# Both layers' attention recorded, and its instructions ordered on all five engines by measured durations

## Chip, cores, metric

One core of a Trainium2 chip. The metric is the device time of one execution in microseconds, as the median over runs. Five instruction streams run beside each other: TensorE (PE), VectorE (DVE), ScalarE (ACT), GpSimd (POOL) and SyncE (SP, which here issues the DMAs). Each runs its own instructions in the order in which the program lists them, and semaphores hold an instruction until its inputs are there.

## What is computed

A two-layer transformer trunk over 512 latent tokens and 256 context tokens, width 1024, all in float32. Each layer:

```python
h, hc = modulate(rms_norm(x, norm1)), modulate(rms_norm(ctx, norm1))
na_q, na_k, na_v, gq, gk, gv, ga, gb = split(h @ w_in)        # hc in the same way
ya = na_latent(...)   # 8 heads: 8x16 window on the 64-wide grid plus bias, and all context keys, one softmax
qb, kb = rope(rms_norm(heads(gq)) * q_gain), rope(rms_norm(heads(gk)) * k_gain)
yb = gqa_latent(...)  # 8 query heads on 2 key heads, latent and context keys
x = x + g1 * ((sigmoid(ga) * (ya @ w_pa) + sigmoid(gb) * (yb @ w_pb)) @ w_o)
if not last:          # context queries on context keys, same weights
    ctx = ctx + cg1 * branch_merge(ya_c, yb_c, ...)
x = x + g2 * swiglu(modulate(rms_norm(x, norm2)))             # ctx as well, if not last
```

## The kernel before

Products in float32 are made of three matmuls: each operand is split into a high and a low half (`wh`, `wl` of a weight, `h`, `hl` of the activations), and h by wh, hl by wh and h by wl add up in one PSUM bank (line L384). `wh` is an ACT copy (L369), `wl` the remainder, on POOL or DVE (L371).

`mixing` is one layer's attention: eight grouped-query heads (GQA), then eight neighbourhood heads (NA). Heads go through in items of two query blocks of 128. Of an item of GQA (`gqa_pair`) PE makes scores `sc` (L1040); DVE takes the minimum `m` over a row (L1048; the query is stored negated) and multiplies it by the row's reciprocal norm `r` (L1054, tile `hr`); ACT makes the exponential `p` and its sum (L1056); DVE scales p (L1010); PE transposes it into `tp` (L1066); ACT copies its high half `pth` (L1016) and DVE its low half `ptl` (L1017); PE multiplies both by the values into `y` (L1076), which ACT and DVE bring back (L1027). `ctx_item` does the same for context queries (L1098, L1103), `na_pair` for NA (L1167 to L1203).

`attend` interleaves one item's scores with the transposes and values of the two before it. In the gaps it runs *fillers*: projection blocks of the queries, keys, values and gates (`gq`, `nq`, `nk`, `nv`, `ga`, `gb`), which are PE work without a wait (tile `pj`) and write tiles that later items need (`kg`, `kk` for the GQA keys, `qg`, `q` for the queries, `qh` and `ql` for NA's). A query's rotation (`rope`) is a shuffle `sh`, a product with the sines on POOL (L791), one with the cosines (L792) and a sum on DVE (L793); a head's norm goes over a small power on POOL (`hr`, L807). A `bias` tile is loaded, zeroed in a part and subtracted on POOL (L1491, L1492).

The order of PE's instructions is planned while the program is built: `Flow` keeps a clock of PE and three timelines of ACT, DVE and POOL, on which each step books an estimated span:

```python
RATE = dict(a=(0.06, 0.00083, "a"), e=(0.28, 0.00083, "a"), v=(0.065, 0.00105, "v"), w=(0.065, 0.00058, "v"),
            g=(0.07, 0.00218, "g"), p=(0.0, 0.19, "g"))
```

A step that needs the result yields `Until(t)`, and the planner fills up to t. Numbers per layer stand in `PLAN` (which fillers in which order, hop times, a reserve). In the attention only PE's order is fixed by hand; DVE, ACT, POOL and SP get theirs from the framework's scheduler. The start of the kernel is ordered by hand on all engines, the feed-forward on PE, DVE and ACT.

After the attention, `merge` loads GQA's results back from memory (`yb`, L1555), splits them (`hi` L396, `lo` L397) and multiplies them by `wp` into `pp`; fillers that are left over run between the last values and the first `pp`. Meanwhile the modulation of the second norm is worked out from `crow` and `wmodT`.

## Time and profile before

| | |
|---|---|
| median of 3 runs | 1951.8 us (1947.15 to 1954.22) |
| the profiled execution | 1945.29 us, span 1943.5 us |
| mean granted clock of TensorE | 0.998 |
| PE busy | 1912.1 us, 98% of the span, 12298 instructions |
| DVE busy | 1470.0 us, 76% |
| ACT busy | 943.0 us, 49% |
| POOL busy | 226.6 us, 12% |
| DMA | 210.85 MB |

Stages in time: start to about 60 us, layer 0's attention to 416, its merge and feed-forward to 1130, layer 1's attention to 1452, the rest to 1943.

A row of a busy table or a group has an engine's busy time, the count in x, and the mean of one instruction in ns; "idle" is the time for which the engine stood just before that instruction, with what released it. PE's matmuls overlap, so that a row's own time is longer than the distance to the next one.

### The profile page before, as it was taken

The page shows a single profiled execution, that of the slowest core. Times are in us where ns is not written, and L with a number is a line of the kernel's source. Part 1 is how long each engine was busy: PE and PEld are TensorE (multiplying, and loading weights), DVE is VectorE, ACT ScalarE, POOL GpSimd, SP SyncE. Part 2 cuts the span into 40 slices and gives each one's busy share as a digit, 9 for nine tenths or more (in the row PEclk, how much of TensorE's full clock was granted, in tenths as well). Part 3 has the DMA queues.
Part 4 walks back from the last instruction along what each step waited for, and adds up shares of the span by engine and source line. Part 5 has one row for each costly group of instructions (what it writes and reads, how often), then busy time and mean ns, then how long its engine had stood idle before and what let it go on. Part 6 is the DMA issues. An engine that isn't in the chain of part 4 may idle for free.

```text
span 1943.5 us, 31493 instructions
## 1 busy us (share of the span) xinstructions
PE 1912.1 (98%) x12298; PEld 1775.8 (91%) x12298; DVE 1470.0 (76%) x2802; ACT 943.0 (49%) x1822; POOL 226.6 (12%) x131
## 2 busy tenths in 40 slices
PE   8999999999999999999999998999999999999998
PEld 8989999998899999999999888889988999999998
DVE  7468887769877888786868577888657687877785
ACT  5466666652336533342424346666553355544553
POOL 0332222213300000000000012322300000000000
PEclk9999999999999999999999999999999999999999
DMA  8121112235562233334344411112235532332332
GB/s 328 44 65 48 47 64 63 77 105 182 170 217 87 66 120 122 117 116 133 131 141 143 143 62 55 47 60 64 73 102 173 201 109 77 98 120 88 103 97 83
DMA packets 71669, 210.85 MB, mean 108 GB/s; under 512 B 8544, under 2 KB 10720, under 8 KB 71520
## 3 DMA queue, kind: packets, MB, share of 16 engines
q1 hardware_dynamic: 71520, 208.84, 33.5%
q8 instruction: 96, 1.57, 0.3%
q14 instruction: 53, 0.43, 0.1%
HBM read 196.75 MB, written 6.82 MB: 105 GB/s over the span
## 4 chain that ended last, share of the span: by engine, by line
PE 69%; DVE 4%; issue 1%; ACT 1%; POOL 0%; DMA 0%; DVEq 0%; POOLq 0%; ACTq 0%
PE po L384 21%; PE qu L1740 14%; PE pj L384 11%; PE qv L1740 7%; PE pp L384 4%; PE qc L1740 3%; PE pf L384 3%; PE pv L957 1%; PE sc L1040 1%; PE y L1076 1%; PE tp L1066 1%; PE y L1203 1%; PE sc L1167 1%; PE tp L1191 1%; DVE m L1048 0%
## 5 line engine op out<-in xcount | busy, mean ns | idle before, releaser
L1740 PE MATMUL qu<-r,w 128*128 128x384 f32 (+1 forms) x1872 | 295.9, 310 | 0.3
L1740 PEld LDWEIGHTS qu<-r,w 128*128 128x128 f32 x1872 | 281.0, 190 | 4.9 <-DVE tt L2219 3.7
L384 PE MATMUL pj<-h,wh 128*128 128x512 f32 (+1 forms) x704 | 257.4, 366 | 3.3 <-ACT kg L816 1.7
L384 PE MATMUL pj<-h,wl 128*128 128x512 f32 (+1 forms) x704 | 247.6, 352 | 1.2 <-POOL wl L371 1.2
L384 PE MATMUL pj<-hl,wh 128*128 128x512 f32 (+1 forms) x704 | 247.0, 351 | 0.0
L369 ACT ACTIVATE wh<-wr 128x1024 fp32r<-128x1024 f32 (+1 forms) x131 | 124.6, 954 | 168.9 <-issue 43.5
L1603 ACT ACTIVATE w<-wr 128x512 fp32r<-128x512 f32 x234 | 145.4, 625 | 107.6 <-DVE wr L2183 36.1
L384 PE MATMUL po<-ph,wh 128*128 128x512 f32 (+1 forms) x576 | 197.5, 343 | 0.0
L384 PE MATMUL po<-ph,wl 128*128 128x512 f32 (+1 forms) x576 | 196.9, 342 | 0.0
L384 PE MATMUL po<-pl,wh 128*128 128x512 f32 (+1 forms) x576 | 196.3, 341 | 0.0
L371 POOL TENSOR_TENSOR wl<-wr,wh 128x1024 fp32r<-128x1024 f32 (+1 forms) x67 | 151.0, 2258 | 370.8 <-ACT wh L369 364.7
L1595 DVE SCALAR_TENSOR_TENSOR x<-po,G,x 128x256 f32<-128x256 f32 (+3 forms) x168 | 99.2, 596 | 101.0 <-PE po L384 100.0
L1607 DVE TENSOR_TENSOR w<-wr,w 128x512 fp32r<-128x512 f32 x234 | 159.4, 686 | 11.9 <-ACT w L1603 11.0
L384 PEld LDWEIGHTS pj<-h,wl 128*128 128x128 f32 x704 | 133.3, 189 | 19.7 <-POOL wl L371 1.6
L1740 PE MATMUL qv<-r,w 128*128 128x384 f32 (+1 forms) x936 | 150.7, 310 | 0.3 <-ACT tt L1746 0.3
L384 PEld LDWEIGHTS pj<-h,wh 128*128 128x128 f32 x704 | 133.7, 190 | 17.4 <-ACT kg L816 1.9
L384 PEld LDWEIGHTS pj<-hl,wh 128*128 128x128 f32 x704 | 134.0, 190 | 13.5
L1740 PEld LDWEIGHTS qv<-r,w 128*128 128x128 f32 x936 | 141.2, 190 | 0.5 <-ACT tt L1746 0.5
L1016 ACT ACTIVATE pth<-tp 128x512 fp32r<-128x512 f32 x176 | 103.2, 595 | 65.1 <-PE tp L1066 36.8
L512 POOL TENSOR_TENSOR rs<-rs,expo 128x2 f32<-128x2 f32 (+2 forms) x8 | 6.2, 773 | 1100.4 <-DVE rs L511 1100.4
L1017 DVE TENSOR_TENSOR ptl<-tp,pth 128x512 fp32r<-128x512 f32 x176 | 119.4, 684 | 18.4 <-ACT pth L1016 17.0
L384 PEld LDWEIGHTS po<-ph,wl 128*128 128x128 f32 x576 | 108.3, 188 | 14.3 <-DVE wl L1911 0.4
(255 smaller groups left out, 4325.2 us busy)
## 6 DMA issues: line engine op xcount, KB each, us to landing
wr<-wfi SPq DMA_DIRECT2D x88, 512.0 KB, 3.3
wr<-wmodT SPq DMA_DIRECT2D x84, 512.0 KB, 3.4
wr<-win SPq DMA_DIRECT2D x68, 512.0 KB, 3.3
wr<-wfo SPq DMA_DIRECT2D x64, 256.0 KB, 2.7
wr<-wo SPq DMA_DIRECT2D x26, 512.0 KB, 3.9
wr<-wp SPq DMA_DIRECT2D x32, 256.0 KB, 3.0
x<-x SPq DMA_DIRECT2D x16, 384.0 KB, 6.7
wr<-wmod SPq DMA_DIRECT2D x12, 512.0 KB, 7.6
```

Source lines behind the costliest of these rows:

```text
L369: nc.scalar.activation(hi, raw, AF.Copy)
L371: (eng or nc.gpsimd).tensor_tensor(lo, raw, hi[:].bitcast(F32), op=ALU.subtract)
L384: nc.tensor.matmul(ps[:, : b - a], u[:, c], v[k][:, a:b], start=(k == 0 and i == 0), stop=(k == nk - 1 and i == 2),)
L957: nc.tensor.matmul(ps[:, t * 256 : t * 256 + 256], a[k][:, tok], b[:, c], start=(k == 0 and i == 0), stop=(k == KB - 1 and i == 2))
L1016: nc.scalar.activation(hi, tp, AF.Copy)
L1017: nc.vector.tensor_tensor(lo, tp, hi[:].bitcast(F32), op=ALU.subtract)
L1040: nc.tensor.matmul(s[:, lo:up], qt[:, b * P : (b + 1) * P], kk[k][:, lo:up], start=(k == 0 and (b % 2 == 0 or lo > 0)), stop=(k == 1), ski ...
L1066: nc.tensor.transpose(tp[:, (2 * j + b) * P : (2 * j + b + 1) * P], ps_[b][:, (k + j) * P : (k + j + 1) * P], self.ident)
L1595: self.nc.vector.scalar_tensor_tensor(x[j][:, f:u], ps[:, f - a : u - a], self.G[l][i][:, s, j : j + 1], x[j][:, f:u], op0=ALU.mult, op1=A ...
L1603: self.nc.scalar.activation(t[:, :n], src, AF.Copy)
L1607: self.nc.vector.tensor_tensor(t[:, n : 2 * n], src, t[:, :n].bitcast(F32), op=ALU.subtract)
L1740: nc.tensor.matmul(banks[bank], u[:, c], v, start=(first and k == 0 and i == 0), stop=(k == kn - 1 and i == 2), skip_group_check=True)
```

## The change

Both layers get `all=True`. Then every instruction that the attention issues goes through a proxy into a list (`Plan.add`) in place of the program. For each instruction the list holds its engine, a cost from measured durations (`cost`, `HOPS` between engines, `TAIL` for overlap), and which earlier instructions it must follow, found from the regions of tiles that it reads and writes; a PSUM bank counts as one region, so two uses of one bank by different engines follow each other. `Flow` takes the ends from these records instead of `RATE` (`Plan.go`). When all is recorded, `emit` runs a simulated list scheduler: PE and SP keep the recorded order; among DVE's, ACT's and POOL's ready instructions the one with the earliest due time goes first, where due times are reckoned back from PE's planned starts. A DVE instruction of the kinds tensor_tensor, tensor_scalar and copy without an operand in PSUM (`shared`) starts no earlier than POOL is free; a POOL instruction is put off when such a DVE instruction with an earlier due time would fall into it. Then the instructions are issued by planned start, and their order holds on all five engines.

Besides, m times r moves from DVE to ACT (64 single products in `gqa_pair`; 8 double ones become 16 in `ctx_item`), in `ctx_item` the scaling of p comes after both exponentials, and the rotation is booked when it is recorded. The numbers in `PLAN` stay.

```diff
+         busy=12, ctx=0.0, vat=(1, 1), load=2, qt=2, rx=2, slow=(1.1, 1.2, 1), banks="gst", lead=(2, 1, 2), quiet=0.0, spared=0, all=True),
...
     def go(self, t, *ops):
+        if self.plan:
+            return self.plan.go(t, ops)
...
+    def passed(self, v):
+        self.clock = max(self.clock + v, self.plan.pe if self.plan else 0.0)
...
+    def __getattr__(self, op):
+        run = getattr(getattr(self._engines.nc, self._name), op)
+        plan = self._engines.plan
+        return (lambda *a, **k: plan.add(self._name, op, run, a, k)) if plan else run
...
+    HOPS = dict(p=0.055, v=0.035, a=0.035, g=0.078, s=0.1)
+    TAIL = dict(p=-0.16, v=0.085, a=0.105, g=0.07, s=-2.2)
...
+    def go(self, t, ops):
+        flow, seen = self.flow, set()
+        for e, n in ops:
+            fixed, each, on = RATE[e]
+            if on in self.recent:
+                t = max(t, self.recent.pop(on))
+                seen.add(on)
+            elif on not in seen:
+                t += 0.05 + fixed + 0.08 + n * each
+        return t + flow.hop - 0.05
...
+        return (0, P, f // S * S, -(-g // S) * S) if psum else (p, p + ap.ap[0][1], f, g)
...
+    def cost(self, lane, op, aps, kw, psum):
+        n = self.size(aps[0])
+        scaled = hasattr(kw.get("scale"), "ap") + hasattr(kw.get("bias"), "ap")
+        if lane == "p":
+            wide = op != "transpose" and aps[1].dtype == F32
+            return max(0.05, 4 * n * PASS / P) if wide else max(PASS, FIX + n * 0.4167e-3)
+        if lane == "s":
+            return n * aps[0].ap[0][1] * 4 / 0.34e6
+        if lane == "g":
+            return 0.31 if op == "memset" else 0.5 + n * 0.142 if n <= 16 else 0.14 + n * 0.0022
+        if lane == "a":
+            return 0.16 + n * 0.00088 + 0.08 * scaled + 0.1 * ("accum_out" in kw)
+        if op == "tensor_reduce":
+            n = self.size(aps[1])
+        one = not psum and op in ("tensor_scalar", "tensor_copy", "reciprocal") and n > 16
+        return 0.15 + n * (0.0006 if one else 0.00105) + 0.06 * (op == "scalar_tensor_tensor" and not psum)
...
+        me = len(self.ops)
+        t, after = flow.clock - 6.0, set()
+        uses = [(v.name, self.region(v, b), any(v is o for o in outs), b) for v, b in zip(aps, bank)]
+        for tile, (p, q, f, g), mine, b in uses:
+            for ((p1, q1, f1, g1), wrote), (end, who) in self.parts.get(tile, {}).items():
+                if (mine or wrote or b) and p < q1 and p1 < q and f < g1 and f1 < g:
+                    who = {w for w in who if mine or wrote or self.ops[w]["lane"] != lane}
+                    if who:
+                        t = max(t, max(self.ops[w]["end"] for w in who if w != me) + self.HOPS[lane])
+                        after.update(who)
+        if lane == "p":
+            at = max([flow.clock, self.pe] + [self.ops[w]["end"] + self.HOPS["p"] for w in after if self.ops[w]["lane"] != "p"])
+            end = at + cost - self.TAIL["p"]
+            self.pe = at + cost
+        elif lane == "s":
+            at = max(t, self.dma)
+            self.dma = at + cost
+            end = self.dma + 2.2
+        else:
+            end = flow.lines[lane].take(t, cost - self.TAIL[lane]) + self.TAIL[lane]
+            at = end - cost
+            self.recent[lane] = max(self.recent.get(lane, 0.0), end)
+        self.ops.append(dict(lane=lane, op=op, cost=cost, after=after, run=run, args=args, kw=kw, at=at, end=end,
+                             shared=lane == "v" and not any(bank) and op in ("tensor_tensor", "tensor_scalar", "tensor_copy"),
+                             tiles={u[0] for u in uses}))
...
+        due, frees = [0.0] * n, [[] for _ in ops]
+        for key in room:
+            of = [t for t in self.users if rings.get(t) == key]
+            for t, new in zip(of, of[_Bufs.rings[of[0]][2] :]):
+                for u in self.users[t]:
+                    if u < self.users[new][0]:
+                        frees[u].append(self.users[new][0])
+        for i in reversed(range(n)):
+            o = ops[i]
+            due[i] = o["at"] if o["lane"] == "p" else min(
+                [due[j] - o["cost"] - 0.05 for j in then[i] + frees[i]], default=o["at"] + 15.0)
+        start, end, ready = [None] * n, [0.0] * n, [-9.0] * n
...
+        def begins(i):
+            if left[i]:
+                return None
+            t = max(ready[i], clock[ops[i]["lane"]])
+            for tile in opens[i]:
+                if not room[rings[tile]]:
+                    return None
+                t = max(t, min(room[rings[tile]]) + self.HOPS[ops[i]["lane"]])
+            return max(t, clock["g"] - 0.07) if ops[i]["shared"] else t
...
+        def put_off(i, t):
+            o = ops[i]
+            for u, j in sorted(soon):
+                if u < t + o["cost"] and due[j] < due[i] and u + ops[j]["cost"] + o["cost"] < due[i]:
+                    t = max(t, u + ops[j]["cost"])
+            return t
...
+            for e in "pavgs":
+                some = queue[e][:1] if e in queue else can[e]
+                times = [(t, i) for i in some for t in (begins(i),) if t is not None]
+                if e == "g":
+                    times = [(put_off(i, t), i) for t, i in times]
+                if times:
+                    first = min(times)[0]
+                    d, t, i = min((due[i], t, i) for t, i in times if t <= first + 0.1)
+                    if e in "av":
+                        for u, j in times:
+                            took = ops[j]["cost"]
+                            if due[j] < d and u < t + ops[i]["cost"] and due[i] > u + took:
+                                d, t, i = due[j], u, j
+                    if best is None or (t, i) < best[:2]:
+                        best = t, i, e
...
+            t, i, e = best
+            o = ops[i]
+            start[i] = t
+            end[i] = t + o["cost"] - min(self.TAIL[e], 0.0)
+            clock[e] = t + o["cost"] - max(self.TAIL[e], 0.0)
+            if e == "a" and o["kw"].get("accum_out") is not None and not exp:
+                exp = True
+                clock[e] += 1.28
+                end[i] += 1.28
...
+        for i in sorted(range(n), key=lambda i: (start[i], i)):
+            ops[i]["run"](*ops[i]["args"], **ops[i]["kw"])
...
         def exp(s, b, at):
             m = ms[b]
             c = 2 * b + v
-            nc.vector.tensor_tensor(m[:, 0:1], m[:, 0:1], r[:, c : c + 1], op=ALU.mult)
+            nc.scalar.activation(m[:, 0:1], m[:, 0:1], AF.Copy, scale=r[:, c : c + 1])
             p = pool.tile([P, T], F32, tag="p", name=self.name("p"))
             nc.scalar.activation(p, s[:, :T], AF.Exp, bias=m[:, 0:1], scale=nr[:, c : c + 1], accum_out=m[:, 1:2])
             self.soften(p, m[:, 1:2], pool)
             ps_.append(p)
-            end = self.go(("v", 1), ("e", T), at=at)
+            end = self.go(("a", 1), ("e", T), at=at)
...
                 rr = r[:].rearrange("p (t v) -> p v t", v=2)[:, v, 4:6]
-                nc.vector.tensor_tensor(m[:, 0:2], m[:, 0:2], rr, op=ALU.mult)
+                for b in range(2):
+                    nc.scalar.activation(m[:, b : b + 1], m[:, b : b + 1], AF.Copy, scale=rr[:, b : b + 1])
...
-            with tc.manual_schedule(engines={mybir.EngineType.PE}):
+            if PLAN[l]["all"]:
+                nc.plan = flow.plan = Plan(flow)
                 flow.run(self.attend(items))
+                nc.plan = None
+                every = ("PE", "DVE", "Activation", "Pool", "SP")
+                with tc.manual_schedule(engines={getattr(mybir.EngineType, e) for e in every}):
+                    flow.plan.emit()
+            else:
+                with tc.manual_schedule(engines={mybir.EngineType.PE}):
+                    flow.run(self.attend(items))
```

The recorded instructions all carry line L541 in the changed kernel. PE's 8660 rows are the same work as before, in another order at 88 places; DVE has 72 instructions fewer, ACT 80 more.

First place: DVE in layer 1's GQA part, when the rotation of the last query block (`qg`) is made. The rows of before (`p` and `rc` scale an exponential, `m` are minima):

```order
L790 STREAM_SHUFFLE sh_13039<-qg_12693 128x512
L1017 TENSOR_TENSOR ptl_12855<-tp_12849,pth_12854 128x512
L1054 TENSOR_TENSOR m_12882<-m_12882,hr_11986 128x1
L1017 TENSOR_TENSOR ptl_12904<-tp_12898,pth_12903 128x512
L1054 TENSOR_TENSOR m_12884<-m_12884,hr_11986 128x1
L792 TENSOR_TENSOR qg_12693<-qg_12693,cos_sb 128x512
L1009 RECIPROCAL rc_12889<-m_12882 128x1
L793 TENSOR_TENSOR qg_12693<-qg_12693,sh_13039 128x512
L1010 TENSOR_SCALAR p_12887<-p_12887,rc_12889 128x768
L1027 TENSOR_TENSOR y_12832<-y_12910,ys_12923 64x256
```

The same stretch of the changed kernel, from the product with the cosines to the sum:

```order
L541 TENSOR_TENSOR qg_11996<-qg_11996,cos_sb 128x512
L541 RECIPROCAL rc_12044<-m_12041 128x1
L541 TENSOR_SCALAR p_12043<-p_12043,rc_12044 128x768
L541 RECIPROCAL rc_12046<-m_12042 128x1
L541 TENSOR_SCALAR p_12045<-p_12045,rc_12046 128x768
L541 TENSOR_TENSOR ptl_12054<-tp_12052,pth_12053 128x512
L541 TENSOR_TENSOR ptl_12057<-tp_12055,pth_12056 128x512
L541 TENSOR_REDUCE m_12059<-sc_12058 128x1
L541 TENSOR_TENSOR ptl_12067<-tp_12065,pth_12066 128x512
L541 TENSOR_REDUCE m_12060<-sc_12058 128x1
L541 TENSOR_TENSOR qg_11996<-qg_11996,sh_12096 128x512
```

Shuffle, cosine product and sum stood within eight rows; now items' work lies between each two of them (the shuffle is twelve rows ahead of the first row shown), and the products of m are gone.

Second place: ACT in the same part of layer 1, before:

```order
L1056 ACTIVATE p_12967,m_12962<-sc_12953,m_12962,nr_12270 128x768
L1024 ACTIVATE ys_13003<-y_12990 64x256
L1056 ACTIVATE p_12973,m_12964<-sc_12953,m_12964,nr_12270 128x768
L1016 ACTIVATE pth_13011<-tp_13006 128x512
L369 ACTIVATE wh_13164<-wr_13162 128x1024
L1530 ACTIVATE gt_13018<-pj_12866 128x512
L1016 ACTIVATE pth_13025<-tp_13020 128x512
L1016 ACTIVATE pth_13074<-tp_13069 128x512
L1056 ACTIVATE p_13058,m_13053<-sc_13044,m_13053,nr_12270 128x768
```

And in the changed kernel:

```order
L541 ACTIVATE pth_12007<-tp_12006 128x512
L541 ACTIVATE m_12000<-m_12000,hr_11843 128x1
L541 ACTIVATE m_12001<-m_12001,hr_11843 128x1
L541 ACTIVATE p_12002,m_12000<-sc_11999,m_12000,nr_11844 128x768
L541 ACTIVATE p_12004,m_12001<-sc_11999,m_12001,nr_11844 128x768
L541 ACTIVATE ys_12010<-y_12009 64x256
L541 ACTIVATE pth_12013<-tp_12012 128x512
L541 ACTIVATE wh_11994<-wr_11993 128x1024
L541 ACTIVATE pth_12016<-tp_12015 128x512
```

The two products of m now stand on ACT right ahead of their exponentials, which follow each other.

Third place: SP, which issues the DMAs, at the end of layer 0's attention (`wr` are weights, `crow` the modulation's vectors), before:

```order
L360 DMA wr_5179<-wmodT 128x1024
L360 DMA wr_5212<-wp 128x512
L360 DMA wr_5218<-wmodT 128x1024
L1555 DMA yb_5104<-yd_0_638 128x768
L1555 DMA yb_5106<-yd_1_639 128x768
L1555 DMA yb_5108<-yd_2_640 128x768
L1555 DMA yb_5110<-yd_3_641 128x768
L437 DMA crow_5169<-crow 128x1024 x2
```

And in the changed kernel:

```order
L632 DMA wr_5187<-wmodT 128x1024
L632 DMA wr_5220<-wp 128x512
L709 DMA crow_5177<-crow 128x1024 x2
L632 DMA wr_5226<-wmodT 128x1024
L1851 DMA yb_5112<-yd_0_638 128x768
L1851 DMA yb_5114<-yd_1_639 128x768
L1851 DMA yb_5116<-yd_2_640 128x768
L1851 DMA yb_5118<-yd_3_641 128x768
```

The two crow loads and a weight now stand ahead of the four loads of yb. Between PE's last values of the layer and its first `pp` stand 102 projection matmuls (54 of 256 columns, 48 of 512) where 75 stood (48 and 27).

More of the change, by code (lines that the diff above doesn't have):

```diff
@@ L225, in fill @@
         else:
-            self.clock += v
+            self.passed(v)
             if f.lead is None:
@@ L908, in gqa_q @@
         end = self.go(("p", n // HD), at=t)
-        end = max(end, self.roped(flow.clock - 1.0))
+        if not flow.plan:
+            end = max(end, self.roped(flow.clock - 1.0))
         nr = self.small.tile([P, 16], F32, tag="hr", name=self.name("nr"))
@@ L912, in gqa_q @@
         self.rope(qg, pool)
+        if flow.plan:
+            end = max(end, self.go(("v", S), at=flow.clock))
         yield Until(end - self.plan["soon"])
```

160 lines of the change are left out of this document (143 added, 17 removed).

## The prediction

> **What bounds the kernel now.** I read the page's busy line and chain first, then a table of windows by stage, then PE's waits inside the two attention stretches.
>
> ```profile
> PE 1912.1 (98%) x12298; PEld 1775.8 (91%) x12298; DVE 1470.0 (76%) x2802; ACT 943.0 (49%) x1822; POOL 226.6 (12%) x131
> PE 69%; DVE 4%; issue 1%; ACT 1%; POOL 0%; DMA 0%; DVEq 0%; POOLq 0%; ACTq 0%
> ```
>
> PE is busy for 98% of the span and carries the chain. The change leaves PE's 8660 rows the same work, so time can only come out of the places where PE stands or limps. The windows (start:end length, then busy us and count of each engine, granted clock, DMA share, GB/s) say where they are:
>
> ```profile
> 60.00:471.00 411.00, 406.50 (x2800) 374.33 (x2799) 314.67 (x674) 235.22 (x500) 116.29 (x62) 1.00 0.24 76
> 633.00:1130.00 497.00, 496.63 (x2853) 471.70 (x2852) 386.74 (x660) 193.92 (x342) 1.01 (x1) 1.00 0.39 123
> 1130.00:1180.00 50.00, 48.14 (x258) 41.41 (x258) 38.31 (x76) 23.41 (x45) 11.90 (x7) 1.00 0.21 64
> 1180.00:1280.00 100.00, 94.28 (x623) 83.63 (x622) 78.03 (x166) 63.20 (x124) 27.42 (x15) 1.00 0.16 49
> 1280.00:1510.00 230.00, 227.47 (x1402) 202.96 (x1401) 164.28 (x353) 122.81 (x249) 40.01 (x23) 0.99 0.32 96
> ```
>
> The feed-forward stretch (633 to 1130) loses 0.4 us of 497. Layer 0's attention loses 4.5 of 411, and layer 1's (1130 to 1510) 10.1 of 380. The granted clock is the same in all of them. PE's waits (engine, line, what it waited for: us, times, longest) in layer 0's attention, then in layer 1's:
>
> ```profile
> PE pj L384 <- POOL wl L371: 1.2, 1, 1.2
> PE pj L384 <- DVE ql L991: 1.1, 2, 0.9
> PE tp L1191 <- DVE z L1010: 1.0, 1, 1.0
> PE y L1076 <- DVE ptl L1017: 0.6, 1, 0.6
> PE pv L957 <- DVE ql L991: 0.5, 1, 0.5
> ```
>
> ```profile
> PE sc L1040 <- ACT p L1056: 2.0, 2, 1.7
> PE tp L1066 <- DVE ptl L1017: 1.9, 1, 1.9
> PE pj L384 <- ACT kg L816: 1.7, 1, 1.7
> PE sc L1040 <- DVE kk L1353: 1.4, 1, 1.4
> PE y L1076 <- DVE ptl L1017: 1.0, 2, 0.8
> PE tp L1066 <- DVE p L1010: 0.8, 1, 0.8
> PE st L804 <- DVE y L1027: 0.7, 1, 0.7
> PE y L1203 <- DVE ptl L1017: 0.4, 1, 0.4
> PE pj L384 <- DVE ql L991: 0.2, 1, 0.2
> ```
>
> Nearly all of them end on DVE, and none is longer than 1.9 us. Idle time is not the whole loss, as two neighbours in PE's timeline show:
>
> ```profile
> 1170.45 0.28 PE L384 MATMUL pj<-h,wl 128*128 128x256 f32 x1
> 1172.39 0.38 PE L384 MATMUL pj<-h,wh 128*128 128x256 f32 x1 [1.67 <-ACT kg L816]
> ```
>
> Matmuls overlap: these 256-wide ones start about 0.12 us apart and show 0.28 each. From start to start this wait cost 1.94 - 0.12 = 1.82 us where 1.67 is shown, so I add 0.15 us to each wait. Shorter waits vanish in the overlap and only lengthen a matmul's record. Grouped by form, the first of the three projection matmuls in layer 0's attention, in layer 1's, and in layer 1's merge (1452 to 1500):
>
> ```profile
> L384 PE MATMUL pj<-h,wh 128*128 128x512 f32 x160 | 66.1, 413 | 1.4 <-DVE ql L991 1.1 <-DVE v L967 0.3
> L384 PE MATMUL pj<-h,wh 128*128 128x512 f32 x176 | 73.2, 416 | 0.2 <-DVE ql L991 0.2
> L384 PE MATMUL pj<-h,wh 128*128 128x512 f32 x23 | 9.0, 389 | 0.0
> ```
>
> Between attention items the same matmul takes 24 to 27 ns more: 160 x 0.024 + 176 x 0.027 = 8.6 us. The other forms (scores, values, narrow projections) are about as many, so I allow them as much, less some 2 us that the restarts hold already: an estimate of 15 us of hidden loss, half in each layer. Weight loading points the same way: 471.70 of 497 is 94.9% in the feed-forward, against 91.1% (60 to 471), 82.8%, 83.6% and 88.2%. The Trainium skill ("Perfetto Trace Analysis", Identifying the Most-Contended Engine) says that matmul busy time misleads because matmuls are pipelined, and that the busy share of weight loads is the better measure; by it, bringing every window to 94.9% would be worth 16 + 6 + 11 + 15 = 48 us, an upper estimate, since the small score and transpose matmuls have another ratio. The trace agrees with it in kind: the visible 14.6 us are not all.
>
> **The change, part by part.**
>
> *PE's visible waits after the start.* Layer 1: 1.9 + 1.0 + 0.8 + 0.7 + 0.4 + 0.2, and 0.3 of the score wait (2.0 - 1.7), 5.3 us; with nine restarts of 0.15, 6.7 us. Layer 0: 1.1 + 1.0 + 0.6 + 0.5 and 0.3 (the projection row's v), 3.5, with six restarts 4.4 us. These are places where DVE does something else first. The clearest is the stretch at 1246 to 1251, where DVE ran the last query block's rotation in one run between two items, and GpSimd stood in its way. DVE's and GpSimd's timeline there, and at the start of the layer:
>
> ```profile
> 1248.01 2.32 POOL L1492 TENSOR_TENSOR bias<-bias 128x768 f32<-128x768 f32 x1 [0.66 <-DMA bias<-rpb]
> 1248.74 2.15 DVE L793 TENSOR_TENSOR qg<-qg,sh 128x512 f32<-128x512 f32 x1
> 1177.22 2.40 POOL L371 TENSOR_TENSOR wl<-wr,wh 128x1024 fp32r<-128x1024 f32 x1
> 1177.29 2.48 DVE L1331 COPY rx<-hr 128x256 f32<-128x256 f32 x1 [1.18 <-POOL hr L807]
> ...
> L793 DVE TENSOR_TENSOR qg<-qg,sh x4: 683/692/2146, 1145.2 to 1248.7; 128x512 f32<-128x512 f32 x4
> ```
>
> Both DVE instructions end 0.1 to 0.6 us after GpSimd's: they stood behind it (the last row has qg's min/median/max in layer 1: 0.69 us is usual).  The new order leaves nine rows between the rotation's product with the cosines and its sum, three low halves (ptl) and two p among them, so the waits for ptl, p and y there (2.3 us) should go. An order from measured durations should remove most such places and can't remove those for which no filler is left: I take 5 of 6.7 and 3 of 4.4. Bounds: 0 (each comes back elsewhere) and all 11.1.
>
> *Start of layer 1* (kg 1.7, kk 1.4, p 1.7: 4.8 us). There DVE is 38.31 busy in 50 us and PE has nothing else to run, so an order moves little: the norm's rows now stand ahead of kg and kk on DVE, which delays one projection and frees a later one. I take 0, with bounds -2 and +2.
>
> *The 1.2 us for wl* stand at 471, behind the attention, where nothing is reordered: 0.
>
> *The hidden loss*, 15 us. It consists of waits of 0.1 to 0.2 us, shorter than the spread of the planned durations, so I let a third go: -5, bounds 0 and -15.
>
> *The products m by the reciprocal norm* leave DVE (64 + 8 rows) for ACT (64 + 16). Their rows on DVE, who waited for them, and the nearest small instruction on ACT:
>
> ```profile
> L1054 DVE TENSOR_TENSOR m<-m,hr x64: 140/150/2060, 97.0 to 1315.5; 128x1 f32<-128x1 f32 x64
>   ACT p L1056: 21.1, 18
> L990 ACT ACTIVATE qh<-pj 64x64 fp32r<-64x64 f32 x16 | 3.4, 215 | 3.2 <-DVE ql L991 3.0
> ```
>
> DVE is relieved of 72 x 0.15 = 10.8 us plus standstills (the longest 2.06), and ACT gets 80 x 0.215 = 17 us more, at 49% busy. The path from minimum to exponential loses a hop between engines and gains 0.07 us. All of it lies beside PE's work while fillers last: 0, already inside the two rows above; if the cover is gone, ACT's queue is the place, priced as a rival below.
>
> *End of layer 0's attention.* The loads of yb now stand behind two crow loads in SP's queue. Before, PE's last values and the first merge matmul, the last low halves on DVE, and the landing times of the loads:
>
> ```profile
> 415.43 0.40 PE L1125 MATMUL y<-ptl,v 128*128 128x256 f32 x2
> 427.57 0.40 PE L384 MATMUL pp<-hi,wh 128*128 128x512 f32 x1
> 421.03 2.89 DVE L397 TENSOR_TENSOR lo<-yb,hi 128x768 fp32r<-128x768 f32 x3 [1.95 <-ACT hi L396]
> yb<-yd SPq DMA_DIRECT2D x4, 384.0 KB, 6.0
> crow<-crow SPq DMA_DIRECT2D x2, 512.0 KB, 8.7
> ```
>
> 75 projection rows filled 415.67 to 427.57, 0.16 us each; now 102 rows stand there, 16 us. The low halves ended 3.7 us before they were needed. Put behind crow, yb lands at most 8.7 - 6.0 later, and I allow 5 us for their being issued later against the last values; 27 more rows (4.3 us) and the 3.7 make 8.0 of cover against 2.7 + 5 = 7.7. So 0, with bounds 0 and +4, the latter if the delay is half as long again.
>
> *New waits.* Engines whose order is fixed stop behind any instruction whose input is late, and behind it stand the pth or ptl for PE. Between 0 and the 8 us that I let go, nearest to the smaller waits of today: three new ones of 0.35 + 0.15, +1.5.
>
> Sum: -5 - 3 + 0 - 5 + 1.5 = -11.5 us. The profiled execution took 1945.3 us (its span 1943.5 and 1.8 around it), 6.5 under the median of 1951.8. So 1933.8 for such an execution and 1940 for the median: 0.6% less, just over the 0.5% (9.8 us) that a measurement of this kernel can tell from no change.
>
> **The rivals.**
>
> *Nearly all goes.* If the planned order holds on the chip, the visible 6.7 + 4.4, half of the start's 4.8 and most of the hidden 15 go: 11.1 + 2.4 + 13 = 26.5, so 1925. For it speaks the feed-forward, which loses 0.4 us of 497. Against it, DVE is 314.67 of 411 busy there and 386.74 of 497 here, alike, but in attention PE waits for results of its own a few us old, so there is less distance between cause and use. Chance 0.15.
>
> *The stalls only move.* DVE's work shrinks by little, and GpSimd's order of work is as recorded: what the plan avoids holds only as long as GpSimd starts when the plan says. If it doesn't, another instruction stands still, 1.4 to 2 us each (2.15 against 0.69 above). Four such, or new waits as long as the 8 us removed, leave only part of the hidden loss: 1948 to 1953, taken as 1950. The Trainium skill ("SBUF — State Buffer", Who interferes with whom) says that the two share a port which whoever starts first holds for its whole instruction, against DVE instructions in a two-port mode and those with two inputs in SBUF; the rows above agree (2.48 us beside 2.40), and no run shown tells how often GpSimd is the one that is held. Chance 0.18.
>
> *Slower: ACT's queue holds PE.* Each m on ACT waits for a minimum on DVE, and behind it in ACT's fixed order stand pth copies, from which ptl and PE's values follow. The page has the low half's mean:
>
> ```profile
> L1017 DVE TENSOR_TENSOR ptl<-tp,pth 128x512 fp32r<-128x512 f32 x176 | 119.4, 684 | 18.4 <-ACT pth L1016 17.0
> ```
>
> If the minimum comes one low half (0.684 us) later than planned, ACT stands that long; at 32 pairs of score blocks that is 32 x 0.684 = 22 us when no filler covers it, with nothing regained then: 1951.8 + 22 - 8 = 1966, and 1960 where a quarter is covered. It decides from about half of the pairs uncovered (11 us, which eats the forecast's gain). For it: ACT's p waited 21.1 us for m in 18 places already, so the minimum is often late. Against it: PE waited for p only 2.0 us. Chance 0.13.
>
> **How the numbers follow.** The forecast has 0.54: its terms' likely ends give 1930 to 1947, and about 0.38 of the 0.54 lies under 1942.0 (faster by over 0.5%). With 0.15 from the first rival, faster is 0.53. Within 0.5%: 0.16 and the second rival's 0.18, 0.34. Slower: 0.13. The range of 8 in 10 reaches from the first rival's 1925 to 1957, between the second rival and the third.
>
> **What would show it.** In the changed kernel's waits of PE for layer 1, ptl, p and y below 2 us in all, and the start's three waits still 3 to 6 us; PE's busy share from 1180 to 1280 up from 94%; the first projection matmul below 410 ns; no DVE instruction without PSUM above 1.5 us beside GpSimd. Layer 0's attention should end about 4 to 6 us earlier, layer 1's 6 to 9 us beyond that. I am wrong if pp waits at the merge, if scores wait for p on ACT by more than 5 us, or if standstills go and PE's stretch is as long as before.

## The result: 1.5% slower, and the profile after

The changed kernel takes 1978.4 us (median of 4 runs, 1977.3 to 1980.1) where the kernel before took 1949.5 (1944.2 to 1954.2) beside it: a ratio of 1.0149, 95% interval 1.0123 to 1.0174. The forecast was 1940, with a range of 1925 to 1957. The profiled execution took 1979.1 us, its span is 1977.3.

The page's busy line and chain of the changed kernel:

```profile
PE 1923.5 (97%) x12298; PEld 1777.8 (90%) x12298; DVE 1463.0 (74%) x2730; ACT 962.6 (49%) x1902; POOL 225.6 (11%) x131
PE 85%; DVE 8%; ACT 3%; issue 2%; DMA 1%; SPq 1%; POOL 0%; DVEq 0%; POOLq 0%; ACTq 0%
```

The same number of matmuls and, within 2 us, the same time of weight loads: no work was added. Of the 33.8 us by which the span grew, PE stands for 22.4 (53.8 us for 31.4). The windows that answer to the four of before (later stages start 20 us later):

```profile
60.00:480.00 420.00, 402.28 (x2732) 365.60 (x2731) 299.14 (x623) 244.76 (x546) 112.57 (x61) 1.00 0.22 70
640.00:1140.00 500.00, 499.32 (x2837) 473.28 (x2836) 390.78 (x677) 197.81 (x357) 1.01 (x1) 1.00 0.38 122
1190.00:1290.00 100.00, 90.79 (x597) 81.49 (x596) 77.19 (x139) 63.04 (x137) 20.14 (x10) 0.97 0.11 36
1290.00:1540.00 250.00, 239.90 (x1457) 209.79 (x1456) 170.35 (x357) 133.97 (x273) 52.34 (x31) 1.00 0.32 100
```

Layer 0's attention loses 17.7 of 420 us now (4.5 of 411 before), the feed-forward loses as little as it did, and layer 1's windows are worse too. PE's waits in layer 0's attention, and in layer 1's from its first scores on:

```profile
PE sc L541 <- DVE m L541: 11.4, 11, 1.4
PE tp L541 <- DVE z L541: 2.9, 2, 1.5
PE sc L541 <- ACT p L541: 1.6, 3, 0.8
PE pj L541 <- DVE ql L541: 0.9, 2, 0.7
PE tp L541 <- DVE rc L541: 0.6, 2, 0.4
```

```profile
PE sc L541 <- DVE m L541: 10.0, 11, 1.1
PE tp L541 <- DVE z L541: 2.9, 3, 1.4
PE sc L541 <- ACT p L541: 2.6, 6, 0.9
PE sc L541 <- DVE kk L541: 0.9, 1, 0.9
```

Many waits of before are gone: not one for ptl or y is left, and in layer 1 none for p on DVE. In their place stands one that did not exist, scores waiting for a minimum: 21.4 us in 22 places. The first of them, from PE's and DVE's timeline:

```profile
93.67 1.32 PE L541 MATMUL sc<-kk,q 128*128 128x512 f32 x7
95.03 0.96 DVE L541 TENSOR_REDUCE m<-sc 128x1 f32<-128x768 f32 x1 [0.38 <-PE sc L541]
96.04 0.49 PE L541 MATMUL sc<-kk,q 128*128 128x512 f32 x1 [1.05 <-DVE m L541]
```

An item's scores are eight matmuls, four for each of its two query blocks. Seven run, then PE stands for the whole minimum over the first block, and only then does the eighth follow, which belongs to the second block. By the code the minimum reads columns 0 to 767 of the score tile and the eighth matmul writes columns 1024 to 1535: neither needs the other, and in the plan's own regions of 512 columns they don't even share a bank. Of the 22 places 19 are of this kind (18.8 us): 11 at the eighth score matmul of a GQA item, 8 in the middle of an NA item. The other three (2.6 us) stand ahead of an NA item's first score matmul.

Stages tell where the time is, in each run below. The table has, from the profiled executions, the time from the first scores (sc from kk) of a layer to its first merge matmul (pp), from there to layer 0's last value of the feed-forward (qv), and from that to layer 1's first scores; and the medians of the timed runs with the ratio to the kernel before beside them.

| kernel | attention 0 | merge, FFN 0 | start 1 | attention 1 | median us | ratio to before |
|---|---|---|---|---|---|---|
| before | 334.1 | 645.6 | 111.6 | 267.3 | 1949.5 | |
| changed | 354.9 | 644.2 | 112.7 | 280.4 | 1978.4 | 1.0149 (1.0123 to 1.0174) |
| e1 PE written ahead | 352.4 | 644.2 | 112.6 | 269.2 | 1963.3 | 1.0070 (1.0048 to 1.0092) |
| e2 before, m on ACT | 339.6 | 652.6 | 111.6 | 268.7 | 1959.0 | 1.0044 (1.0026 to 1.0061) |
| e3 e1, m on DVE | 348.4 | 644.3 | 112.8 | 275.9 | 1969.0 | 1.0098 (1.0080 to 1.0116) |
| e4 e1, bias early | 345.8 | 644.1 | 111.2 | 266.5 | 1959.2 | 1.0048 (1.0031 to 1.0066) |
| e5 e1, standstills not counted | 347.2 | 646.7 | 112.7 | 271.7 | 1965.8 | 1.0080 (1.0059 to 1.0100) |
| e7 e4, slack 0.5 | 338.7 | 650.8 | 113.4 | 264.5 | 1957.2 | 1.0030 (1.0015 to 1.0046) |
| e8 e4, PE's order alone | 358.2 | 646.4 | 112.7 | 271.7 | 1977.2 | 1.0137 (1.0123 to 1.0151) |
| e9 e4 in layer 1 alone | 334.2 | 648.8 | 111.1 | 265.4 | 1951.2 | 1.0002 (0.9991 to 1.0013) |
| e10 e4, banks not counted | 348.8 | 644.0 | 111.3 | 267.5 | 1960.8 | 1.0052 (1.0038 to 1.0067) |
| e11 e9, slack 0.5 | 334.0 | 650.3 | 113.4 | 264.5 | 1948.2 | 0.9984 (0.9969 to 0.9998) |
| e12 e4, slack 1.0 and 0.5 | 338.2 | 650.0 | 111.9 | 262.4 | 1956.2 | 1.0035 (1.0020 to 1.0050) |

After layer 1's first pp all of them take the same 442.5 us to the last qv. The table leaves out the time before layer 0's first scores, which start at 92.8 to 96.7 us.

The profiles' granted clocks lie between 0.992 and 0.998. What is missing from 1 lies in single stretches of 3.41 or 6.83 us in which the clock is half. Outside the last 60 us of the kernel each of them begins while PE stands for 1.0 to 3.8 us, or at most 1.4 us after that. In e1 one reaches from 287.3 to 294.1, behind a wait of 3.0 us. Matmuls of 256 columns start 0.213 us apart in it, and 0.120 behind it:

```profile
292.34 0.41 PE L546 MATMUL pj<-h,wl 128*128 128x256 f32 x1
292.56 0.41 PE L546 MATMUL pj<-h,wh 128*128 128x256 f32 x1
...
294.34 0.28 PE L546 MATMUL sc<-k,ql 128*128 128x256 f32 x1
294.46 0.28 PE L546 MATMUL sc<-k,qh 128*128 128x256 f32 x1
```

So by estimate 3.41 us at half clock cost PE up to 1.5 us (3.41 x (1 - 0.120 / 0.213)), and 6.83 us up to 3.0, on top of the wait. Not every wait is followed by such a stretch: one of 3.3 us in e4 isn't. In layer 0's attention there is none before, 3.41 us in the changed kernel, 10.24 in e1, 6.83 in e2, e3 and e8, and none in the others. In layer 1's there are 3.41 us before, in the changed kernel, e2, e8 and e10, 6.83 in e5, 10.24 in e3, and none in the others. A stage's difference of 1 to 3 us can thus be one such stretch. With PE's shown waits, 0.15 us for each restart and these stretches taken off, little is left between the versions: 643.9 to 644.9 us for merge and feed-forward, 255.9 to 259.4 for layer 1's attention, and for layer 0's 329.7 before, 332.9 in the changed kernel, 333.7 in e1 and at most 336.8 (e10).

### The profile page after: what moved, and what is told of

Its sections match the earlier page's. It is cut to its first block, busy times and chain, and to the rows that moved or that the text cites. A ratio compares the mean times of both kernels' runs of the same rounds, so it can differ in the third digit from the quotient of the medians.

```text
span 1977.3 us, 31456 instructions
## 1 busy us (share of the span) xinstructions
PE 1923.5 (97%) x12298; PEld 1777.8 (90%) x12298; DVE 1463.0 (74%) x2730; ACT 962.6 (49%) x1902; POOL 225.6 (11%) x131
## 4 chain that ended last, share of the span: by engine, by line
PE 85%; DVE 8%; ACT 3%; issue 2%; DMA 1%; SPq 1%; POOL 0%; DVEq 0%; POOLq 0%; ACTq 0%
PE po L656 21%; PE qu L2036 13%; PE pj L541 10%; PE qv L2036 7%; PE pj L656 6%; PE pp L656 6%; PE pv L541 3%; PE qc L2036 3%; PE sc L541 3%; PE y L541 3%; PE tp L541 3%; PE pf L656 3%; DVE m L541 2%; ACT p L541 1%; PE pj L952 1%
## 5 line engine op out<-in xcount | busy, mean ns | idle before, releaser
L541 PE MATMUL pj<-h,wh 128*128 128x512 f32 (+1 forms) x512 | 189.5, 370 | 3.3 <-ACT kg L541 2.3
L541 PE MATMUL pj<-h,wl 128*128 128x512 f32 (+1 forms) x512 | 179.0, 350 | 0.0
L541 PE MATMUL pj<-hl,wh 128*128 128x512 f32 (+1 forms) x512 | 178.7, 349 | 0.0
L641 ACT ACTIVATE wh<-wr 128x1024 fp32r<-128x1024 f32 (+1 forms) x85 | 75.9, 898 | 126.2 <-PE po L656 31.8
L541 DVE TENSOR_TENSOR ptl<-tp,pth 128x512 fp32r<-128x512 f32 x176 | 118.8, 685 | 24.3 <-ACT pth L541 22.0
L541 POOL TENSOR_TENSOR wl<-wr,wh 128x1024 fp32r<-128x1024 f32 x44 | 105.7, 2411 | 213.7 <-ACT wh L541 213.7
L541 ACT ACTIVATE pth<-tp 128x512 fp32r<-128x512 f32 x176 | 102.6, 596 | 54.2 <-PE tp L541 52.6
L656 PEld LDWEIGHTS po<-pl,wh 128*128 128x128 f32 x576 | 108.6, 188 | 12.8
L656 PEld LDWEIGHTS po<-ph,wh 128*128 128x128 f32 x576 | 108.6, 188 | 12.7
L724 DVE CUSTOM_DVE_ANT_0 wr<-wr,crow 128x1024 f32<-128x1024 f32 x80 | 100.8, 1260 | 13.6 <-DMA wr<-wmodT 12.8
```

The lines of the kernel that those rows point to most:

```text
L541: ops[i]["run"](*ops[i]["args"], **ops[i]["kw"])
L641: nc.scalar.activation(hi, raw, AF.Copy)
L656: nc.tensor.matmul(ps[:, : b - a], u[:, c], v[k][:, a:b], start=(k == 0 and i == 0), stop=(k == nk - 1 and i == 2),)
L724: self.nc.vector.tensor_tensor_reduce(junk if s else w, w, crow[:, s], 1.0, 0.0, ALU.mult, ALU.add, self.mod[l][:, s, n : n + 1])
```

## The experiments

**e1, the same orders, PE written earlier.** A plan fixes the order on each engine, but the program is one list, and the framework makes waits from that list: an instruction waits for what stands ahead of it and touches the same tile. `emit` writes by planned start, and the minimum starts in the plan between the seventh and the eighth score matmul. In the program of the changed kernel the eighth matmul of 11 of the 32 latent GQA items carries a wait for DVE, and so do score matmuls in the middle of some NA items; in before's program no such wait stands on the eighth matmul of a GQA item. The edit writes PE's instructions up to 1 us of planned time earlier, as far as their own inputs allow; each engine's order stays the same row for row.

```diff
-        for i in sorted(range(n), key=lambda i: (start[i], i)):
+        key, last = list(start), -99.0
+        for i in sorted((i for i in range(n) if ops[i]["lane"] == "p"), key=lambda i: (start[i], i)):
+            if not opens[i]:
+                key[i] = min(start[i], max([last, start[i] - 1.0] + [start[w] + 1e-6
+                             for w in ops[i]["after"] if ops[w]["lane"] != "p"]))
+            last = key[i]
+        for i in sorted(range(n), key=lambda i: (key[i], i)):
```

> The changed kernel; each engine keeps its own order row for row, but a recorded PE instruction is written into the program up to 1 us of planned time ahead of the other engines' instructions that it doesn't depend on. With that the last score matmul of 11 GQA items and one of some 8 NA items no longer waits for DVE (the waits on the minimum of the same item). Theory A, the slow-down is made by these waits, which exist only because the minimum was written between two score matmuls of one item: PE's waits of scores on m fall from 21.4 us (22 times) to under 5, and the time from 1978 by 21.4 + 22 x 0.15 = 25 us to about 1954 (1950 to 1960). Theory B, DVE's new order makes the minima late, and what PE does not wait for at the scores it waits for at the next transposes: 1970 to 1978, with waits of tp or y on DVE up by 15 us or more.

1963.3 us, 15.1 less than the changed kernel. The minimum's wait shrinks from 21.4 to 1.5 us. What PE waits for most in layer 0, then in layer 1:

```profile
PE tp L546 <- DVE rc L546: 4.0, 3, 3.0
PE tp L546 <- DVE z L546: 2.9, 2, 1.4
PE sc L546 <- ACT p L546: 1.8, 3, 1.0
PE sc L546 <- DVE m L546: 1.3, 2, 0.7
...
PE sc L546 <- ACT p L546: 4.5, 7, 0.9
PE tp L546 <- DVE z L546: 3.6, 3, 1.5
```

The time lies between the ranges of the two theories. Theory A holds for the cause: the waits came from where an instruction was written, since nothing else was changed, and in the two traces every engine's rows follow each other in the same order. The three waits that stand ahead of an item's first score matmul are the ones that stay. In layer 1 all of it came back (280.4 to 269.2 us). In layer 0's attention only 2.5 us did (354.9 to 352.4): PE's waits fell from 17.5 to 12.0 us, since something else is late there and PE waits for that instead, which is B's part; and 6.83 us more ran at half clock, which took back up to 3.0.

**e2, the small edit alone**, beside the old order: `exp` and `ctx_item` as in the change's diff, all else as before.

> The kernel before, with only the small edit: m times r as ACT copies with a scale in gqa_pair and ctx_item (80 on ACT in place of 72 on DVE), the rest ordered as before by the scheduler. Theory A gives this edit no part in the slow-down: 1942 to 1954, no change. Rival, ACT's queue (0.29 us for each product where DVE took 0.15, and pth behind it): 5 to 10 us slower than before, 1955 to 1960, with waits of scores on p or of y on ptl up by as much.

1959.0 us, slower by 0.26 to 0.61%: the time is the rival's. The price of a product on ACT was also mis-sized. The changed kernel's row:

```profile
L541 ACT ACTIVATE m<-m,hr x80: 279/294/302, 96.1 to 1334.7; 128x1 f32<-128x1 f32 x80
```

0.29 us, where I had taken 0.215 from a 64x64 copy without a scale from a tile. The Trainium skill ("ScalarE: Activation LUTs", What ACT_TABLE_LOAD costs) gives 186 ns plus 0.833 ns for each element and about 93 ns for each operand that is a column of a tile. By these figures an estimate for this product is 280 ns, and the trace agrees within 5%. In e2's profile 5.5 of the added us are in layer 0's attention, up to 3.0 of them 6.83 us at half clock at a wait of 1.8 us for ptl. Another 7.0 are in the merge behind it, which the rival did not name. Nothing was edited there, and by names and shapes the instructions of the merge and the feed-forward stand in the same order on every engine as before (waits of e2 there):

```profile
PE po L384 <- DVE wl L371: 3.6, 2, 2.6
PE pj L384 <- POOL wl L371: 1.9, 1, 1.9
PE po L384 <- ACT mh L1590: 1.2, 1, 1.2
```

**e3, the small edit undone in e1.**

> The kernel of e1 (PE written ahead) with the small edit undone: m times r again as one DVE product. Theory A, the ACT copies (0.29 us each and a longer way from minimum to exponential) make p late, as e2 showed beside the old order: 5 to 8 us under e1's 1963, so 1955 to 1958, and PE's waits of scores on p (6.3 us in e1) under 3. Theory B, in this order it makes no difference since DVE loses what ACT gains: 1961 to 1966.

1969.0 us, 5.7 more than e1, so neither: in the planned order the products are better on ACT. Layer 0's attention is 4 us faster with them on DVE, layer 1's 6.7 slower (waits of tp for z and y there 3.9 and 2.1 us). Of these, up to 1.5 and 4.5 us are stretches at half clock, by their length. The edit's sign is another here than in e2.

**e4, the bias of two heads at once.** In e1 the start of NA in layer 0 loses most. Its timelines there (SP, POOL, DVE, PE):

```profile
270.77 0.33 SPq L546 DMA_DIRECT2D yd<-y  x1
273.96 0.58 SPq L546 DMA_DIRECT2D bias<-rpb  x1
278.25 1.84 POOL L546 TENSOR_TENSOR bias<-bias 128x768 f32<-128x768 f32 x1 [27.40 <-DMA bias<-rpb]
280.12 0.69 DVE L546 CUSTOM_DVE_ANT_1 z<-sc,bias 128x512 f32<-128x512 f32 x1 [4.68 <-POOL bias L546]
283.66 2.35 POOL L546 TENSOR_TENSOR wl<-wr,wh 128x1024 fp32r<-128x1024 f32 x1 [3.57 <-ACT wh L546]
284.52 2.02 DVE L546 TENSOR_SCALAR z<-z,rc 128x512 f32<-128x512 f32 x1
286.69 0.41 PE L546 MATMUL tp<-ident_sb,z 128*128 128x128 f32 x2 [3.01 <-DVE rc L546]
```

The second head's bias stands in SP's queue behind the store yd of the last GQA pair and four NA query copies, and is issued 36 us after the first one. Before, the scheduler had put it ahead of the store:

```profile
239.30 0.54 SPq L1489 DMA_DIRECT2D bias<-rpb  x1
248.85 0.33 SPq L1477 DMA_DIRECT2D yd<-y  x1
```

So POOL is late, DVE stands 4.7 us, and the z that follow meet GpSimd's wl, which they should have avoided (2.02 us, until 0.5 us after wl's end).

```diff
-                if head not in bias:
-                    t = bias[head] = ...
+                for hd in (head, head | 1):
+                    if hd in bias:
+                        continue
+                    t = bias[hd] = ...
```

> The kernel of e1, with the bias of an odd NA head loaded and subtracted together with that of the even head before it, so that in layer 0 the second head's bias stands ahead of the store of the last GQA pair in SP's queue. Theory C, SP's recorded order (a store that waits for the last GQA values stands ahead of the second bias) makes POOL, DVE's z and PE late at the start of NA: the waits at 281 to 289 in e1 (0.6 + 3.0 + 1.4 us, with the small ones around them 6 to 8) go and the time is 1955 to 1958. Theory D, GpSimd's instructions are only shifted and meet DVE elsewhere: 1960 to 1966, with waits of tp on rc or z still 8 to 10 us.

1959.2 us, 4.1 less, between the two theories' ranges and with overlapping intervals. The waits are theory C's: from 255 to 300 us those on rc, z and m (5.0 us) became 0.4. But a projection now waits 3.3 us there for DVE's k, ahead of which a scaling of p took 2.45 us. By stage layer 0's attention gains 6.6 us and layer 1's 2.7. Up to 4.5 of the 6.6 are the 10.24 us at half clock, which are gone in e4's profile. The profiled executions are e1's longest and e4's shortest; e1's shortest took 1957.4 us at a clock of 0.999, e4's two shortest 1956.8 and 1957.7 at 0.998. So the late bias is shown as the cause of these waits, and its 4.1 us aren't clear of noise.

**e5, standstills not counted**: `shared=False` in e1.

> The kernel of e1, where the plan no longer holds DVE instructions back while GpSimd is busy (shared is False for all, which also ends the putting off of GpSimd). Theory E, the counted standstills are not where the time goes, since GpSimd on the chip starts at other times than planned: within 3 us of e1, 1960 to 1966. Rival, they are what helped DVE: 5 to 10 us slower, 1968 to 1973. Other rival, holding DVE back costs: 1953 to 1958.

1965.8 us, 2.5 above e1 with overlapping intervals, as theory E had it. Counting them hardly matters, and it does not keep DVE clear of GpSimd. The scaling of p over 768 columns, as the mean of 64, before, in e1 and in e5:

```profile
L1010 DVE TENSOR_SCALAR p<-p,rc 128x768 f32<-128x768 f32 x64 | 41.2, 644 | 2.0
...
L546 DVE TENSOR_SCALAR p<-p,rc 128x768 f32<-128x768 f32 x64 | 44.4, 694 | 1.9
...
L546 DVE TENSOR_SCALAR p<-p,rc 128x768 f32<-128x768 f32 x64 | 43.8, 684 | 1.9
```

**e6, the kernel before once more.**

> The kernel before, once more with a profile. Its times lie between 1943 and 1954 and the first profile fell at 1945.3; in e2's profile the merge of layer 0 took 7 us longer (waits of po on wl). If that is a thing of single executions and not of the edit, this profile, if it falls near 1952, shows it too.

It fell at 1945.1 us with the same stages to 0.2 us, so it says nothing on executions near 1952. e9 and e11 say more: their layer 0 is that of before, and from its first pp to its last qv their rows, and those of e2 and e12, stand on every engine in the order of before, by names and shapes. They still take 3 to 7 us longer there, with po waiting for wl. So this time isn't one of order; what starts it stays open.

**e7, slack for PE's order.** Before, `Flow` stretched bookings by 1.1 and 1.2 and added hops; `Plan.go` gives bare recorded ends.

```diff
-        return t + flow.hop - 0.05
+        return t + flow.hop - 0.05 + 0.5
```

> The kernel of e4, with 0.5 us added to every end that the planner of PE's order is told (Plan.go); the simulated order of the other engines is then made for that PE order. Theory F, the recorded ends are bare durations, where the booked ones of before were stretched (1.1 and 1.2) and had hops, so PE comes to scores, transposes and banks before they are free: waits of scores on p (about 6 us in e4) fall under 2, those of tp too, and the time by 5 to 9 us, to 1950 to 1954. Rival, the waits come from what stands ahead on DVE and POOL and slack only shifts fillers: 1957 to 1962.

1957.2 us, the lower edge of the rival's range, and 2.0 less than e4 with overlapping intervals. In layer 0's attention theory F holds: 345.8 to 338.7 us, PE's waits from 10.3 to 3.9, and those that are left are small:

```profile
PE sc L546 <- ACT p L546: 1.3, 2, 1.0
PE pj L546 <- DVE ql L546: 1.1, 2, 0.7
PE tp L546 <- DVE rc L546: 1.0, 2, 0.7
```

But the merge behind it takes 6.7 us longer (650.8 for 644.1). That is one wait of a projection for the eviction of t, 3.8 us, and up to 3.0 for the 6.83 us at half clock that begin in it:

```profile
PE pj L661 <- DVE t L1890: 3.8, 1, 3.8
```

**e8, only PE's order imposed**: `every = ("PE",)` in e4, the other engines left to the scheduler.

> The kernel of e4, where only PE's recorded order is imposed; DVE, ACT, POOL and SP are ordered by the framework's scheduler (which changes 231 rows of DVE, 181 of ACT, 21 of POOL, 36 of SP). Theory H, the order made for DVE, ACT and POOL is what loses in layer 0: 1949 to 1954, near the kernel before. Rival, PE's new order (theory F's missing slack) loses whoever orders the others: 1957 to 1964.

1977.2 us, 18 more than e4 and above both ranges: the opposite of theory H. The order made for DVE, ACT, POOL and SP is better than the scheduler's for this PE order; the scheduler serves it worse than PE's order of before. Its largest waits in layer 0's attention:

```profile
PE pj L546 <- DVE ql L546: 7.0, 4, 2.3
PE sc L546 <- ACT p L546: 6.0, 7, 1.6
PE tp L546 <- DVE ptl L546: 3.1, 3, 2.0
```

**e9, layer 1 alone.** Layer 0 gets `all=False`, the product on DVE and the bias one by one.

> Layer 0 as before, layer 1's attention recorded and ordered as in e4. By the stages of e4's profile layer 1 takes 266.5 us from its first scores to its first merge matmul where 267.3 were taken before, and its start 0.4 us less: 1949 to 1952, no change against before's 1951.4 (theory: all of what is left of the slow-down is in layer 0). Rival: 1955 or more, if layer 1 loses elsewhere.

1951.2 us, ratio 1.0002: all that is left in e4 comes with layer 0's edit. Layer 1's attention is 1.9 us faster than before by stage, up to 1.5 of it the stretch at half clock that followed a wait of 1.9 us before.

**e10, banks not counted.** In e4 a PSUM tile's region is its columns, and two readers don't order each other.

```diff
-        uses = [(v.name, self.region(v, b), any(v is o for o in outs), b) for v, b in zip(aps, bank)]
+        uses = [(v.name, self.region(v, False), any(v is o for o in outs), False) for v, b in zip(aps, bank)]
```

> The kernel of e4, where the plan takes a PSUM tile's columns as they are and no longer a whole bank as one region (2072 rows of PE's order move). Theory F: the counted banks only made the planned ends later and so left PE a little slack; without them PE comes still earlier to banks in use, 1962 to 1975, with more waits of scores and transposes on DVE and ACT. Rival, the counting forbids orders that the chip allows: 1950 to 1957.

1960.8 us, within the intervals of e4 (1959.2) and between both expectations: no effect that can be told, with PE's order changed in 2072 rows.

**e11, e9 with e7's slack.**

> The kernel of e9 (layer 0 as before, layer 1 recorded and ordered), with the 0.5 us of slack of e7. In e7's profile layer 1 went from its first scores to its first merge matmul in 264.5 us, in e9's in 265.4, before in 267.3; the start took 2 us more in e7 than in e9. So 1948 to 1952, at best 0.1% under before's 1950 to 1951. Rival: the slack takes PE's waits away as in layer 0 (7 us there): 1942 to 1946.

1948.2 us, 0.02 to 0.31% under the kernel before, as expected: the only version whose interval lies below it, and barely. Layer 1 took the forecast 264.5.

**e12, more slack in layer 0** (1.0 us there, 0.5 in layer 1).

> The kernel of e7 with 1.0 us of slack in layer 0 and 0.5 in layer 1. Theory F has layer 0's attention (345.8 us in e4's profile without slack, 338.7 with 0.5, 334.1 before) at 334 to 337 now, and the time at 1950 to 1955 if the merge behind it takes the 644 to 651 us it took so far. Rival, the first half microsecond took what slack can give, and more only leaves fillers for the end: 338 to 342 for the stage, 1955 to 1960.

1956.2 us, and 338.2 us for layer 0's attention: both are the rival's. The second half microsecond gave 0.5 us. Against before, layer 0's attention is 4.1 us longer; PE's shown waits there add up to 6.4 us, the longest 1.7, where they were 3.5 before.

## Why the prediction was wrong

*The step that failed is "New waits", three of 0.35 us, +1.5.* The waits for a minimum alone were 21.4 us in 22 places, and with 0.15 us for each restart 24.7. I asked which instruction would be late; at 19 of these places none was. A minimum written between two score matmuls in the program gave PE a wait that has no data behind it. Taking this away by e1 was worth 15.1 us net, half of the loss of 28.9.

*The second failure is what "New waits" did not ask of the DMA queue.* I followed SP's queue at the end of layer 0's attention, where nothing happened (no wait of pp), and not at the start of NA, where the recorded order put a store ahead of the second bias: 5.0 us of waits in e1, and 4.1 us by e4's median, with overlapping intervals.

*A cost that no term holds is the clock.* I read it as the same in all windows, and the last one showed 0.99: 3.41 us at half clock, from 1285.4 on, behind a wait of 1.9 us. A wait was priced at its length and 0.15 us; with such a stretch behind it, it costs up to 1.5 or 3.0 us more. From the first scores of layer 0 to the first pp of layer 1 the changed kernel has three such stretches where before had one, by their length up to 3 us of the loss.

*"Hidden loss", -5, did not come at all.* The first projection matmul was to fall under 410 ns. In layer 0's attention and in layer 1's it takes 416 and 420 in the changed kernel, where it took 413 and 416 before:

```profile
L541 PE MATMUL pj<-h,wh 128*128 128x512 f32 x160 | 66.6, 416 | 0.2 <-DVE ql L541 0.2
L541 PE MATMUL pj<-h,wh 128*128 128x512 f32 x133 | 55.9, 420 | 0.0
```

What is left of layer 0's attention without waits, restarts and half clock grew by 3.2 us, and of layer 1's by 3.0, instead of shrinking. By the Trainium skill's measure, the busy share of weight loads ("Perfetto Trace Analysis", Identifying the Most-Contended Engine), the estimate of what could be gained was 48 us. No version here got any of it: the weight loads' busy time stayed between 1774 and 1783 us in all of them, and their share only followed the span.

*"PE's visible waits", -5 and -3: right in their own places, and outweighed.* Layer 1's waits for ptl, p and y, below 2 us as predicted, are 0. But tp for z and scores for p, 5.5 us, are as much as those that went. Without the written-in waits layer 1 is at 266.5 (e4) to 264.5 us (e7, e11), 1 to 3 us better than before where I had said 5, and up to 1.5 us of that is the stretch at half clock. In layer 0 no version with the new order came under 338.2, where 334.1 were taken before.

*"Start of layer 1", 0: right* (112.7 for 111.6). *The 1.2 us at 471* went with the shift.

*The products on ACT, 0: the term is larger than its zero, with both signs.* Alone they cost 5 to 12 us (e2), in the planned order they save 5.7 (e3).

*The slower rival had the sign and not the mechanism.* It had ACT stand for late minima and hold pth: PE's waits for p on ACT are 4.2 us in 9 places, and for pth none is shown. It had a chance of 0.13 and a time of 1960 to 1966; that the time rose beyond this is no merit of it. *The rival that GpSimd doesn't keep to the plan* is seen in e1 and e5: counted or not, the scaling of p over 768 columns takes as long (694 and 684 ns). The edit of e5 changes 2.5 us with overlapping intervals; what the standstills themselves cost isn't shown.

In sum, of 28.9 us the waits from the written order are 15.1 (e1). The bias behind a store (4.1, e4) and the missing slack (2.0, e7) are seen in the waits, but neither median is clear of noise alone. The rest, some 8 us, comes with layer 0's new order as well, since without it nothing is left (e9). By e12's profile it is 4.1 us in layer 0's attention, 4.4 in the merge behind it and 2.9 ahead of the first scores, where layer 1's attention gives 4.9 back; what adds the time in the merge isn't the order there. For the attention's part e8 points to PE's order; which of its 88 places does it stays open.

## What to carry to other kernels

When a plan reorders several engines, the order in which the instructions of different engines are written is part of the plan: waits are made from it. List the waits that the new program gives to the bottleneck engine and compare them with the old ones; one that names an engine whose result isn't used can be read before any run. Price a wait with what the clock does behind it. Keep slack between a planned end and the bottleneck engine's use of it, and follow each recorded queue, the DMA queue too, past every store that waits.

## What the runs showed of the hardware

A one-column product on ACT with its scale from a tile takes 0.29 us, twice DVE's 0.15. DVE's scaling of z, without PSUM, took 2.02 us beside GpSimd's wl (2.35 us) and ended 0.5 us after it, where its median is 0.49, as the rows of before had shown for other kinds of instruction. Stands of PE of 1.0 to 3.8 us were in several cases followed by 3.41 or 6.83 us at half clock, in which matmuls of 256 columns start 0.213 us apart in place of 0.120. And executions of one kernel differ by some 0.5%, the longer ones mostly at a lower granted clock: the kernel before took 1943.4 us at 0.999 and 1954.4 at 0.996.
